# Key and query projections as seven half-size products, and another schedule for the modulation columns, in an encoder layer on one core

## The chip, the cores and the metric

The kernel runs on one core of a Trainium2 chip. The metric is the device time of one execution in microseconds (us). A profiled execution comes with it: a trace of every instruction, and a page that sums it up. Engines: PE multiplies matrices (PEld loads its stationary operand), DVE is the vector engine, ACT the scalar engine, POOL is GpSimd, SP issues loads.

## The reference, cut to what matters

One layer on 512 tokens of width 1024: a SwiGLU block (FFN1), a mixer, a second SwiGLU block (FFN2). Each begins with an RMS norm whose output is scaled and shifted by vectors made from `c`.

```python
mod = c_act @ w_mod[l] + b_mod[l]
(sh1, sc1, g1, sh2, sc2, g2, sh3, sc3, g3) = jnp.split(mod, N_MOD, axis=-1)
...
h = modulate(rmsnorm(x, norm_mix[l]), sh2, sc2)
qa, ka, va, qb, kb, vb, ga, gb = jnp.split(h @ w_in[l], SPLIT_POINTS, axis=-1)
...                                     # attention A: windowed, on qa, ka, va
qb = apply_rope(rmsnorm(qb.reshape(B, S, B_HEADS, 2, HEAD_DIM), qn_b[l]), cos, sin)
kb = apply_rope(rmsnorm(kb.reshape(B, S, B_HEADS, 2, HEAD_DIM), kn_b[l]), cos, sin)
ob = diff_attention(qb, kb, vb, lam)    # attention B: dense, difference of two softmaxes
...
merged = jax.nn.sigmoid(ga) * ya + jax.nn.sigmoid(gb) * yb
x = x + g2[:, None, :] * (merged @ w_out[l])
```

## The kernel before

All products are done in three passes: each float32 operand is split into a high and a low part (`split_from`, line 190: a cast on ACT and a subtraction on DVE), and high x high, high x low and low x high are added up in PSUM. A weight tile is 128 x 1024 (512 KB); it comes into one of five `raw` buffers, and its parts go to one of five slots of two large tiles, `high` and `low` (`high_low`). For some weights the low part is made otherwise: ACT writes minus the high part, and a load from POOL's queue adds the weight to it (`load_main`).

**FFN1 and FFN2** use Winograd's form of Strassen's scheme, in class `Unit`: a product of 2 x 2 blocks with seven products of half size in place of eight. Four differences of h blocks (`h_sum`: `n1`, `n2`, `t3`, `t4`) and three sums of weight blocks are needed; the latter are made by accumulating loads on POOL's queue. Each product (`a11`, `a12`, `s1`, `s2`, `s3`, `s4`, `a22`) is 4 chunks x 2 halves x 3 matmuls of 256 columns (`two`, lines 458 to 460). `Unit.after` copies and adds the products to the four result blocks `c11`, `c12`, `c22`, `c21` and hands each to `post`. `run_items` runs a list of such products, and asks for and splits their weights some products ahead (`ASK`, `MAKE`).

**The modulation vectors** are made in columns of 128 values: a 512 KB load of `w_mod`, and one multiply-and-reduce on DVE (`mod_col`, line 283). `column` loads one and computes the one loaded two or so calls before. 24 columns (`rest`) run beside FFN1, a column whenever `SIDE` = 0.27 an item has added up to 1; 24 (`later`) beside the mixer's projections, one in four steps; 8 (`latest`) beside the last product of the mixer.

**The mixer** begins with `boundary`: the end of FFN1, the norm in two halves (`hidden`, lines 354 to 363) and three gates' products with their matmuls. Then `main()` yields PE's steps one by one: the projections of B's values, keys and queries (`project`, lines 1202 to 1204: 8 chunks x 4 blocks of 128 tokens x 3 matmuls of 512 columns each), two gates, A's keys, values and queries (`project_pairs`), the other gates (`gates`) until attention B is done, then A's start, the remaining gates and the branches. Beside these steps an object `line` runs the attention's pieces when their estimated time is due (`line.at`, `line.helped`): norm and rotation of the heads (`head_stats`, `rope`), their turning on PE (`turn_heads`, four transposes), scores (`diff_scores`), softmax differences, outputs. The first scores of B wait for the second turned block of queries. The engines' order in the mixer is chosen by the scheduler of the programming layer, by program order and an estimate of what is ready; in other stages the order of some engines is as written (`manual_schedule`).

Of the kernel before, what the change touches and what calls it, by code (L numbers as in the profile page):

```python
# [11 lines left out]
F32 = mybir.dt.float32  # L12
# [100 lines left out]
EARLY, NEXT, SIDE, LATER = 3, 3, 0.27, 4  # L113
# [21 lines left out]
def layer(ctx: ExitStack, tc: tile.TileContext, a: dict):  # L135
# [212 lines left out]
    def hidden(rb, c, sc, sh, hi, lo, r=FULL[0], value=None):  # L348
# [3 lines left out]
        if value is not None:  # L352
            rb = rb[:, r]
# [3 lines left out]
        if value is not None:  # L357
            if r.stop - r.start == T:
                t3 = t.rearrange("p (t q) -> p t q", t=2)
            else:  # L360
                t3 = t.unsqueeze(1)
            S.activation(value, t3, AF.Identity, bias=s)
# [9 lines left out]
    def boundary(parts, g, norm, sc, sh, hh, hl, into, ahead, at):  # L372
# [16 lines left out]
        def h_steps(rs, r):  # L389

            before = None
# [69 lines left out]

    class Unit:
# [15 lines left out]
        in_order, by_columns, asides = (), (), {}  # L478
# [17 lines left out]
        def prepare(self, q):  # L496
# [8 lines left out]
            else:  # L505
                hi, lo = high_low(n, self.asides.get(q, ASIDE), (self, q))
# [9 lines left out]
        def multiply(self, q, ks=None):  # L516
# [6 lines left out]
            for js in ((0,), (1,)) if q in self.by_columns else (range(2),):  # L523
                for k in ks:
                    x = self.operand(OPERAND[q], k)
                    two(po, self.ready[q], k, x, new and k == 0, k == self.depth - 1, js)
# [22 lines left out]
    def run_items(items):  # L549

# [21 lines left out]
        for n, (u, q, ks, also) in enumerate(items):  # L572
# [3 lines left out]
            u.multiply(q, ks)  # L576
# [25 lines left out]
    def h_sum(t):  # L602
# [4 lines left out]
        h_op[t] = [u4() for _ in range(2)] if t == "n1" else b8()  # L607
# [3 lines left out]
        for i in range(2):  # L611
            v = hq[t][:, i * T : (i + 1) * T].rearrange("p (k q) -> p k q", k=2)
            o = h_op[t][i] if t == "n1" else h_op[t][:, 2 * i : 2 * i + 2, :]
# [223 lines left out]
    rest, later, latest = rest[: EARLY * NC], rest[EARLY * NC : (EARLY + NEXT) * NC], rest[(EARLY + NEXT) * NC :]  # L837
# [117 lines left out]
    def item1(u, q, ks=None):  # L955
        items1.append((u, q, ks, side1))

    credit, asked = [0.0], []
# [13 lines left out]
    def side1(n=SIDE):  # L972

        while small_loads and len(rest) < 20:
# [150 lines left out]
    def load_main(src, aside=0):  # L1125

        raw = sbuf("raw", [P, 1024], F32, RAW)
        nc.sync.dma_start(raw, src)
# [41 lines left out]

    vb_w = boundary(
# [19 lines left out]
    def project(srcs, n, then):  # L1191
# [3 lines left out]
        for u in range(NC // per):  # L1195
            wh, wl = srcs.pop(0) if isinstance(srcs, list) else load_halves(srcs[u])
# [54 lines left out]
    def head_stats(raw, nh, rs, scale8):  # L1251

        sq = f2()
        n = nh * HD
        S.activation(sq[:, 0:n], raw, AF.Square)
        V.tensor_reduce(rs, sq[:, 0:n].rearrange("p (h d) -> p h d", d=HD), axis=AX.X, op=ALU.add)
        if scale8:
            V.tensor_scalar(rs, rs, HD * EPS, None, ALU.add)
        else:
            V.tensor_scalar(rs, rs, 1.0 / HD, EPS, ALU.mult, ALU.add)  # L1260
        G.tensor_tensor(rs, rs, half[:, 0:nh], ALU.pow)
        return sq

    def rope(raw, nh, tabs, t, z):
        C, R = tabs
        n = nh * HD
        y = f2()
        r3 = raw.rearrange("p (h d) -> p h d", d=HD)
        y3 = y[:, 0:n].rearrange("p (h d) -> p h d", d=HD)
        z3 = z[:, 0:n].rearrange("p (h d) -> p h d", d=HD)  # L1270
        V.tensor_tensor(y3, r3, C[:, t, :].unsqueeze(1).broadcast_to([P, nh, HD]), ALU.mult)
        for o, i in ((slice(0, NF), slice(NF, HD)), (slice(NF, HD), slice(0, NF))):
            V.tensor_tensor(z3[:, :, o], r3[:, :, i], R[:, t, o].unsqueeze(1).broadcast_to([P, nh, NF]), ALU.mult)
# [845 lines left out]
```

## Time and profile before

| | |
|---|---|
| median of 3 runs | 1034.36 us (1034.01 to 1039.83) |
| profiled execution | 1034.51 us, its span 1032.7 us |
| PE busy | 1027.6 us, 7346 matmuls |
| DVE busy | 787.4 us |
| ACT busy | 582.1 us |
| POOL busy | 161.8 us |
| moved by DMA | 220.39 MB |
| mean granted clock of PE | 0.999 |

The span goes from the first to the last instruction; the execution's time holds some 2 us around it. FFN1 lies at 0 to 340 us, the boundary to 373.6, values, keys and queries to 439.9, attention B from 466 to 563, attention A from 570 to 641, FFN2 from 709 on.

### The profile page before, as it was taken

The numbers are of one execution on the slowest core, as the hardware profiler recorded it, in microseconds if no ns is written. First come the engines' busy times: TensorE is split into PE (matmuls) and PEld (weight loads), VectorE is DVE, ScalarE is ACT, GpSimd is POOL, SyncE is SP. The second block draws the span as 40 slices with busy tenths as digits, with TensorE's granted clock in tenths as the row PEclk, the third lists the DMA queues.
The fourth block names the chain that finished last, engine by engine and source line by source line (L and its number), as shares of the span: only waits on it lengthen the run. The fifth ranks groups of instructions, "written<-read, shape, count | busy, mean of one in ns | idle before, by whom it ended". The sixth has DMA issues, their size and how long they took to land.

```text
span 1032.7 us, 18848 instructions
## 1 busy us (share of the span) xinstructions
PE 1027.6 (100%) x7346; PEld 949.0 (92%) x7346; DVE 787.4 (76%) x1457; ACT 582.1 (56%) x1013; POOL 161.8 (16%) x189
## 2 busy tenths in 40 slices
PE   9999999999999999999999999999999999999998
PEld 7889899899998998899888888989999999999998
DVE  7886667567787679859772588976898777877877
ACT  6755335244454443668785856525877556655553
POOL 1101110110100100543323101001112112212210
PEclk9999999999999999999999999999999999999999
DMA  9977887967875459796737944974498998989974
GB/s 363 371 207 202 239 241 219 251 153 243 218 188 158 144 213 410 237 281 135 181 79 185 259 136 151 367 250 103 93 239 195 238 236 209 222 228 215 207 158 113
DMA packets 70233, 220.39 MB, mean 213 GB/s; under 512 B 8448, under 2 KB 13184, under 8 KB 70144
## 3 DMA queue, kind: packets, MB, share of 16 engines
q1 hardware_dynamic: 47808, 146.52, 39.2%
q0 software_dynamic: 19200, 68.17, 35.9%
q10 hardware_dynamic: 3136, 4.51, 1.2%
q8 instruction: 57, 0.93, 0.4%
q14 instruction: 32, 0.26, 0.1%
HBM read 208.94 MB, written 10.23 MB: 212 GB/s over the span
## 4 chain that ended last, share of the span: by engine, by line
PE 96%; DVE 2%; ACT 2%; issue 0%; POOL 0%; DVEq 0%; ACTq 0%
PE acc L460 7%; PE acc L459 7%; PE acc L458 7%; PE sc L460 6%; PE sc L458 6%; PE sc L459 6%; PE sc L174 5%; PE sc L176 5%; PE sc L175 5%; PE acc L174 5%; PE acc L176 5%; PE acc L175 5%; PE tp L1281 2%; PE acc L709 2%; PE acc L1203 2%; PE acc L1202 2%
## 5 line engine op out<-in xcount | busy, mean ns | idle before, releaser
L190 ACT CAST high<-raw 128x1024 fp32r<-128x1024 f32 (+2 forms) x176 | 158.4, 914 | 149.4 <-PE sc L175 40.8
L190 DVE TENSOR_TENSOR low<-raw,high 128x1024 fp32r<-128x1024 f32 (+2 forms) x176 | 183.5, 1052 | 40.4 <-ACT high L190 38.8
L459 PE MATMUL acc<-b,high 128*128 128x256 f32 x508 | 140.5, 277 | 0.1
L458 PE MATMUL acc<-b,high 128*128 128x256 f32 x508 | 140.6, 277 | 0.0
L460 PE MATMUL acc<-b,low 128*128 128x256 f32 x508 | 140.5, 277 | 0.0
L460 PE MATMUL sc<-b,low 128*128 128x256 f32 x500 | 138.0, 276 | 0.0
L458 PE MATMUL sc<-b,high 128*128 128x256 f32 x500 | 138.0, 276 | 0.0
L459 PE MATMUL sc<-b,high 128*128 128x256 f32 x500 | 138.0, 276 | 0.0
L190 ACT CAST high<-u 128x1024 fp32r<-128x1024 f32 (+1 forms) x73 | 75.4, 1034 | 52.3 <-PE sc L175 20.0
L190 DVE TENSOR_TENSOR low<-u,high 128x1024 fp32r<-128x1024 f32 (+1 forms) x73 | 87.7, 1201 | 21.5 <-ACT high L190 20.0
L174 PE MATMUL sc<-b,high 128*128 128x512 f32 (+1 forms) x272 | 97.4, 358 | 0.0
L175 PE MATMUL sc<-b,high 128*128 128x512 f32 (+1 forms) x272 | 97.0, 357 | 0.0
L176 PE MATMUL sc<-b,low 128*128 128x512 f32 (+1 forms) x272 | 97.0, 357 | 0.0
L459 PEld LDWEIGHTS acc<-b,high 128*128 128x128 f32 x508 | 95.4, 188 | 0.5 <-DVE b L1903 0.3
L458 PEld LDWEIGHTS acc<-b,high 128*128 128x128 f32 x508 | 95.4, 188 | 0.2
L460 PEld LDWEIGHTS acc<-b,low 128*128 128x128 f32 x508 | 95.4, 188 | 0.1
L460 PEld LDWEIGHTS sc<-b,low 128*128 128x128 f32 x500 | 93.9, 188 | 0.0
L458 PEld LDWEIGHTS sc<-b,high 128*128 128x128 f32 x500 | 93.9, 188 | 0.0
L459 PEld LDWEIGHTS sc<-b,high 128*128 128x128 f32 x500 | 93.9, 188 | 0.0
L174 PE MATMUL acc<-b,high 128*128 128x512 f32 (+1 forms) x240 | 89.2, 372 | 0.0
L176 PE MATMUL acc<-b,low 128*128 128x512 f32 (+1 forms) x240 | 86.6, 361 | 0.0
L175 PE MATMUL acc<-b,high 128*128 128x512 f32 (+1 forms) x240 | 86.5, 360 | 0.0
(400 smaller groups left out, 2717.9 us busy)
## 6 DMA issues: line engine op xcount, KB each, us to landing
u<-w_mod SPq DMA_DIRECT2D x38, 512.0 KB, 8.0
b<-w_mod SPq DMA_DIRECT2D x32, 512.0 KB, 5.5
raw<-w2i SPq DMA_DIRECT2D x31, 512.0 KB, 5.6
u<-w2i POOLq DMA_DIRECT2D x31, 512.0 KB, 6.8
raw<-w1u SPq DMA_DIRECT2D x24, 512.0 KB, 6.5
u<-w1u POOLq DMA_DIRECT2D x24, 512.0 KB, 7.1
raw<-w1o SPq DMA_DIRECT2D x24, 384.0 KB, 4.8
raw<-w_gate SPq DMA_DIRECT2D x16, 512.0 KB, 5.4
```

The source lines that it names most:

```text
L174: PE.matmul(out, wh, xh, start=first, stop=False)
L175: PE.matmul(out, wh, xl, start=False, stop=False)
L176: PE.matmul(out, wl, xh, start=False, stop=last)
L190: last = S.copy(hi, src), V.tensor_tensor(lo, src, f(hi), ALU.subtract)
L458: PE.matmul(out, wh[:, s], xh, start=first and j == 0, stop=False, skip_group_check=True)
L459: PE.matmul(out, wh[:, s], xl, start=False, stop=False, skip_group_check=True)
L460: PE.matmul(out, wl[:, s], xh, start=False, stop=last and j == 1, skip_group_check=True)
L709: PE.matmul(out1[i][:, r], w[:, i * P : (i + 1) * P], h[:, r], start=first and r.start == 0, stop=last and r.stop == T, skip_group_check=True,
L1202: PE.matmul(out[t][:, 0:n], hh[k][:, ht], wh[:, o : o + n], start=k == 0, stop=False)
L1203: PE.matmul(out[t][:, 0:n], hh[k][:, ht], wl[:, o : o + n], start=False, stop=False)
L1281: PE.transpose(tp[:, j * P : (j + 1) * P], src, ident)
```

## The change

Two things are changed together.

Keys and queries of attention B become two `Unit`s (`projected`), each with seven products of half size. Here h is the stationary operand and the weight the moving one (`two_turned`). Their weights are laid out in four blocks, whose sums are made by accumulating loads; the four differences of h are made on DVE and ACT beside the values' projection, from f32 values of h that ACT now keeps in the boundary (`hidden` with `value`). The result blocks, two blocks of tokens by four heads, go through `two_blocks` (which attention A used before) in place of `head_stats` and `rope`, and are turned a quarter at a time (`turn_quarter`). The first scores wait for all four key quarters and the first query quarter; later ones for the query quarter that they read. `item_steps` is `run_items` as a generator, so that columns and attention pieces can come between its products' parts. SP's order from the values to the first two gates is as written.

The columns: 32 beside FFN1 at 0.44 an item, none beside the items of the final out products and of the last unit; 4 (`later`) beside the values (one in 8 steps) and the units (one in 14); 12 (`tail`) beside the gates from the tenth turned block of attention B on, one in four steps, into `raw` buffers, with the activated `c` loaded anew into one of these; 8 (`latest`) as before.

```diff
-EARLY, NEXT, SIDE, LATER = 3, 3, 0.27, 4
+EARLY, NEXT, SIDE, LATER = 4, 2, 0.44, (8, 14, 2)
+BESIDE_V = 4
...
             for c in range(NC):
-                h = hidden(rs, c, sc, sh, hh[c], hl[c], r)
+                value = hq[f"b{c // 4 + 1}{n}"][:, c % 4 * H : (c % 4 + 1) * H]
+                h = hidden(rs, c, sc, sh, hh[c], hl[c], r, value)
...
+    def two_turned(po, w, k, x, first, last, js=range(2)):
+
+        (wh, wl), (xh, xl) = w, x
+        s = slice(k * 2 * P, (k + 1) * 2 * P)
+        for j in js:
+            r = slice(j * P, (j + 1) * P)
+            out = po[:, j * H : (j + 1) * H]
+            PE.matmul(out, xh[:, r], wh[:, s], start=first and j == 0, stop=False, skip_group_check=True)
+            PE.matmul(out, xl[:, r], wh[:, s], start=False, stop=False, skip_group_check=True)
+            PE.matmul(out, xh[:, r], wl[:, s], start=False, stop=last and j == 1, skip_group_check=True)
...
     def item1(u, q, ks=None):
-        items1.append((u, q, ks, side1))
+        ended = u.final if isinstance(u, Out1) else u.p == NH - 1
+        items1.append((u, q, ks, lambda: side1(0.0 if ended else SIDE)))
...
-            w = room[len(columns) % len(room)] if columns is not later else None
-            asked.append((v, c, mod_load(v, c, w)))
+            w = None
+            if columns is tail:
+                w = sbuf("raw", [P, 1024], F32, RAW)
+            elif columns is not later:
+                w = room[len(columns) % len(room)]
+            with tc.issue_after(loaded[0]) if columns is tail else nullcontext():
+                asked.append((v, c, mod_load(v, c, w)))
         if asked and (len(asked) > COLUMNS[columns is rest] or not columns):
-            mod_col(*asked.pop(0), in_order=columns is not later)
+            after = summed[0] if columns is later else split[1] if columns is tail else None
+            with nullcontext() if after is None else tc.issue_after(after):
+                mod_col(*asked.pop(0), in_order=columns is rest or columns is latest)
...
+    def projected(w, post, odd):
+        u = Unit([w[i] for i in range(4)], 4, h1_operand, post, odd)
+        u.srcs = dict(zip(("a11", "a12", "a21", "a22"), u.srcs))
+        u.products, u.aside = two_turned, -ASIDE
+        u.in_order = ("s1", "s2", "s3", "s4", "a22")
+        return u
...
+    key_unit.ask("s1")
     vb_w = boundary(
...
+    def keys_b(c, v, u):
+        n, i, raw = quarter(c, v)
+        rs = small(8)
+        y = two_blocks(raw, 4, table["kb"], i, rs.rearrange("p (t h) -> p t h", t=2), False)
+        y3 = y.rearrange("p (h d) -> p h d", d=HD)
+        V.tensor_tensor(y3, y3, rs.unsqueeze(2).broadcast_to([P, 8, HD]), ALU.mult)
+
+        def turn():
+            turn_quarter(y, n, i, kb_h, kb_l)
+            keys_done.add((n, i))
+
+        line.at(line.helped(3.2, 4.0) + SLACK, turn, ("tp",))
...
     def main():
-        yield from beside(project(vb_w, T, values_b), LATER)
-        yield from beside(project(a["w_kb"], T, keys_b), LATER)
-        yield from beside(project(a["w_qb"], T, queries_b), LATER)
-        yield from beside(gates(lambda: gate_next[0] < EARLY_A), 1)
+        with tc.manual_schedule(engines={mybir.EngineType.SP}):
+            k, q = key_unit, query_unit
+            with tc.issue_after(split[0]), tc.issue_after(split[1]):
+                k.prepare("s1")
+            h_sum("n1", False)
+            for t in ("n2", "t3", "t4"):
+                h_sum(t, False)
+            summed.append(split[1])
+            for p in ("a11", "a12"):
+                k.ask(p)
...
+            yield from beside(project(vb_w, T, values_b, also), LATER[0])
+            items = [(k, p, None, None) for p in ("s1", "a11", "a12", "s2", "s4", "s3")]
+            items += [(q, "s1", None, None), (k, "a22", None, None)]
+            items += [(q, p, None, None) for p in ("a11", "a12", "s2", "s4", "s3", "a22")]
+            yield from beside(item_steps(items, MM3), LATER[1])
+            yield from beside(gates(lambda: gate_next[0] < EARLY_A), LATER[2])
...
-        yield from gates(lambda: done["b"] < NT)
+        yield from gates(lambda: turns["b"] < 10)
+        cact[0] = sbuf("raw", [P, 1024], F32, RAW)
+        with tc.issue_after(loaded[0]):
+            nc.sync.dma_start(cact[0], c_scr.partition_broadcast(P))
+        yield from beside(gates(lambda: done["b"] < NT), 4, tail)
+        while tail or asked:
+            column(tail)
         line.drain(lambda: done["b"] == NT)
         start_a()
```

More of the change, by code (lines that the diff above doesn't have):

```diff
@@ L549, in run_items, with item_steps @@
     def run_items(items):
+        for _ in item_steps(items):
+            pass
+    def item_steps(items, cost=None):
         due, at, now = [], [], 0.0
@@ L1249, in gates @@
             gate_end(j, out)
[L1251 to L1273, printed above, removed]
-        V.tensor_tensor(y[:, 0:n], y[:, 0:n], z[:, 0:n], ALU.add)
-        return y
     def turned(srcs, tag="tp"):
@@ L1287, in cut @@
         return [src[:, j * P : (j + 1) * P] for j in range(n)]
-    def turn_heads(y, nt, t, hi, lo, then=None):
-        ht = slice(t * P, (t + 1) * P)
-        v = turned(cut(y, nt)).rearrange("p (j q) -> p j q", j=nt)
-        with tc.high_priority():
-            split_from(hi[:, 0:nt, ht], lo[:, 0:nt, ht], v)
-        turns["t"] = t + 1
-        if then is not None:
-            line.at(line.free["tp"] + SLACK, then, SCORES)
     def raws(ps, n=T):
```

119 lines of the change are left out of this document (72 added, 47 removed).

## The prediction

> **What bounds the kernel now.** I read the page first: the busy shares and the chain that ended last. Then the waits of the tensor engine (PE), which tell whether a busy PE is also an unhindered one.
>
> ```profile
> span 1032.7 us, 18848 instructions
> PE 1027.6 (100%) x7346; PEld 949.0 (92%) x7346; DVE 787.4 (76%) x1457; ACT 582.1 (56%) x1013; POOL 161.8 (16%) x189
> ...
> PE 96%; DVE 2%; ACT 2%; issue 0%; POOL 0%; DVEq 0%; ACTq 0%
> ```
> ```profile
> PE acc L634 <- DVE sm L640: 0.9, 1, 0.9
> PE acc L187 <- DVE u L190: 0.2, 1, 0.2
> ```
>
> Look at two things: the chain lies on PE for 96% of the span, and the whole list of PE's waits adds up to 1.1 us (one at the start, one near 601 us in the window attention). Busy time alone would not prove that PE streams at its peak, because matmuls overlap. So I take the spacing of their starts, first of the three projections with 512 columns (values, keys, queries in a row), then of matmuls with 256 columns.
>
> ```profile
> 373.61 0.40 PE L1202 MATMUL sc<-high,b 128*128 128x512 f32 x1
> ...
> 439.90 0.39 PE L174 MATMUL acc<-b,high 128*128 128x512 f32 x1
> ```
> ```profile
> 451.63 0.28 PE L1222 MATMUL acc<-high,b 128*128 128x256 f32 x1
> ...
> 453.84 0.28 PE L1223 MATMUL acc<-low,b 128*128 128x256 f32 x1
> ```
> ```profile
> 820.00:880.00 60.00, 60.00 (x531) 60.00 (x531) 46.21 (x68) 33.96 (x49) 11.28 (x13) 1.00 0.93 225
> ```
>
> The code issues 8 chunks x 4 blocks x 3 = 96 matmuls for each projection, so 288 start between 373.61 and 439.90, with two groups of four transposes among them (0.44 us and a little each): (66.29 - 1.1) / 288 = 0.2264 us each. In the last row, of a stretch of FFN2 (columns: PE, PEld, DVE, ACT, POOL, clock, DMA share, GB/s), 531 matmuls of 256 columns touch 60 us, some two of them overhanging: 60 / 529 = 0.1134 us. That is half of 0.2264, with the granted clock at 1.00. Between lie the `L1222` group's rows: from 451.63 to 453.84 are 19 starts, 0.1163 us each. So the kernel is bound by the number of columns that PE streams, and the stage of this change stands in an unbroken stream.
>
> **The change part by part.**
>
> *Seven products for eight.* Removed: keys and queries, 192 matmuls x 0.2264 = 43.5 us. Added: two units of 7 products x 4 chunks x 2 halves x 3 = 168 matmuls of 256 columns, 336 in all. In them h is stationary and the weights move, as in `L1222`, but with the banks and operand tiles of the FFN units. Bounds: 336 x 0.1134 = 38.1 and 336 x 0.1163 = 39.1 us. I take 0.115, between the two, since the trace has both: 38.6 us. That is -4.9 us (bounds -5.4 and -4.4). The transposes stay 32 in number, in eight groups of four.
>
> The Trainium skill ("TensorE: Matmul & The Clock Gate", "Back-to-back issue gap") speaks against this: it gives a sustained spacing of about 81 ns at 128 columns and 131 ns at 512, so short matmuls would pay more for each column. An estimate by that page, 98 ns at 256 columns on the line between, makes 336 x 0.098 = 32.9 us against 192 x 0.131 = 25.2: 7.8 us slower. By that rule, the trace does not agree: 0.1134 is half of 0.2264.
>
> *What DVE and ACT get for it.* The units need four sums of h (two subtractions and two splits on DVE each), 14 weight splits for 8, and 6 additions of the quarters.
>
> ```profile
> 368.47 4.63 DVE L190 TENSOR_TENSOR low<-raw,high 128x1024 fp32r<-128x1024 f32 x4 [0.45 <-ACT high L190]
> ...
> 407.21 1.29 DVE L190 TENSOR_TENSOR low<-raw,high 128x512 fp32r<-128x512 f32 x2
> 408.42 1.28 DVE L283 CUSTOM_DVE_ANT_0 u<-u,ka,par 128x1024 f32<-128x1024 f32 x1
> ```
> ```profile
> 374.00:396.00 22.00, 22.00 (x99) 18.20 (x98) 16.75 (x29) 4.97 (x10) 0.00 (x0) 1.00 1.01 389
> 396.00:418.00 22.00, 22.00 (x99) 18.23 (x98) 19.33 (x38) 7.93 (x16) 0.00 (x0) 1.00 1.03 409
> 418.00:440.00 22.00, 22.00 (x102) 18.18 (x102) 20.45 (x42) 15.55 (x30) 13.19 (x8) 1.00 0.65 199
> 440.00:466.00 26.00, 26.00 (x181) 24.02 (x180) 14.49 (x36) 17.18 (x33) 10.78 (x8) 1.00 1.05 281
> ```
>
> Two 512-wide operations take 1.21 us from start to start (407.21 to 408.42), a full weight split 1.16 (4.63 / 4). Added: 16 x 0.605 = 9.7 for the sums, 14 x 1.16 - 8 x 1.21 = 6.6 for the splits, 6 x 0.605 = 3.6: 19.9 us. Removed from this stretch: 20 of the 24 modulation columns at 1.28, 25.6 us. DVE falls from 71.0 us (the four rows) to about 65, while PE's 92 us fall to 87. So on average DVE has room. Within the units it is tighter; one tile's norm and rotation stand in a row here, an operation of each kind:
>
> ```profile
> 427.23 0.68 DVE L1274 TENSOR_TENSOR f<-f,f 128x512 f32<-128x512 f32 x1
> ...
> 430.36 0.69 DVE L190 TENSOR_TENSOR low<-raw,high 128x512 fp32r<-128x512 f32 x1
> ```
>
> That is 430.36 - 427.23 = 3.1 us, and 0.6 for the split of the turned tile (queries have one multiplication less): 3.7 a key quarter, 3.1 a query quarter. Beside the 38.6 us of products come 11 weight splits (three are made during the values), 12.8; additions, 3.6; the values' own four splits, 2.4; two columns, 2.6; four key and two query quarters, 14.8 + 6.2: 42.4 us. What lags is the rotation, which nothing needs before the first scores. Forecast cost 0.3 us; bounds 0 and 3.8 (all of the overhang shown as PE waits). Queued behind a late split on DVE would be the next split, and behind that PE's next product; behind a late POOL accumulation, the one that turns one weight sum into the next.
>
> ```profile
> u<-w1u POOLq DMA_DIRECT2D x24, 512.0 KB, 7.1
> ```
> ```profile
> 420.38 3.72 POOL L1261 TENSOR_TENSOR sm<-sm,half 128x8 f32<-128x8 f32 x2 [60.33 <-DVE sm L1260]
> ```
>
> Eight accumulating loads join POOL's queue, each 7.1 us to landing by the row of FFN1, among the eight powers of the norms, 1.9 us each (3.72 / 2). The products that read them come at least three products (8 us) after the split that releases them, the spacing at which FFN1 and FFN2 run without a PE wait. Nothing more for them, inside the same bounds. SP's order in this stretch is now the program's, past the loads of the removed columns: at 389 to 409 GB/s they filled the DMA engines, and without 10 MB of them the eight accumulations have room.
>
> *Boundary.* Before the mixer, ACT keeps an f32 value of h too: 16 more activations of 256 columns.
>
> ```profile
> 366.20 0.51 ACT L355 ACTIVATE b<-f,mod 128x256 fp32r<-128x256 f32 x1 [0.28 <-DVE f L354]
> 366.99 0.51 ACT L355 ACTIVATE b<-f,mod 128x256 fp32r<-128x256 f32 x1 [0.28 <-DVE f L354]
> ```
>
> A step takes 0.79 us, ACT is idle for 0.28; a second activation of at most 0.51 makes it at most 1.02, 0.23 x 8 = 1.8 us later at the end of a half. The second half's work goes under the gates' matmuls, and the first weight split of the values ends at 368.47 + 1.16 = 369.6, with 4.0 us to the start of their matmuls at 373.61. The chain through the norm of the second half is shorter of slack. I take 0.3 us, bounds 0 and 1.8.
>
> *Columns.* FFN1 takes 32 for 24, at 0.44 an item for 0.27, and none beside its last out products and its last unit.
>
> ```profile
> 80.00:160.00 80.00, 80.00 (x560) 74.27 (x559) 55.85 (x74) 33.85 (x44) 9.66 (x11) 1.00 0.88 233
> 160.00:240.00 80.00, 80.00 (x563) 74.37 (x562) 54.24 (x70) 33.59 (x43) 7.92 (x9) 1.00 0.71 188
> 240.00:317.00 77.00, 77.00 (x585) 73.22 (x584) 59.82 (x92) 37.79 (x52) 8.48 (x10) 1.00 0.80 227
> ...
> 744.00:798.00 54.00, 54.00 (x479) 54.00 (x478) 50.22 (x82) 38.70 (x67) 11.30 (x13) 1.00 0.95 220
> ```
>
> DVE: 169.9 us of 237, plus 8 x 1.28 = 10.2: 76%. FFN2 has DVE at 50.22 / 54 = 93% and PE unbroken, so this costs nothing; without that cover, 10.2 us is what could show. The loads bring 8 x 0.5 MB, 10 us at 409 GB/s, into a stage whose DMA share is 0.80 on average. Taking columns from FFN1's end gains nothing: no PE wait stands there.
>
> Twelve columns go beside the end of the differential attention: 15.4 us of DVE, and 6.3 MB, 15.4 us at 409 GB/s.
>
> ```profile
> 500.00:535.00 35.00, 34.94 (x215) 28.17 (x215) 27.52 (x73) 30.08 (x78) 12.28 (x18) 1.00 0.47 114
> 535.00:570.00 35.00, 35.00 (x196) 29.50 (x193) 12.47 (x33) 22.13 (x55) 8.85 (x14) 1.00 0.72 174
> ```
>
> DVE has 30 us free in these 70, the DMA engines 28 (0.53 x 35 + 0.28 x 35). They fit; cost 0, and the far end is in the rivals.
>
> *Earlier attention.* The first scores stand at
>
> ```profile
> 466.43 0.74 PE L187 MATMUL sc<-b,b 64*128 64x512 f32 x3
> ```
>
> and need now one query quarter and all keys, ready ten products after the values' end (373.6 + 21.7 + 27.6 = 422.9) plus about 8 us of norm and rotation: near 432. That gives no time by itself (PE had work anyway); it leaves more gate matmuls as cover for the window attention, worth the 0.2 us wait at 601.
>
> **Sum**, against the profiled execution's own 1034.51 us (span 1032.7): 1034.5 - 4.9 + 0.3 + 0.3 - 0.2 = 1030.0 us. The median shown is 1034.36, 0.15 less, so 1029.8.
>
> **The rivals.**
>
> *Gate weights starve (slower).* The tail's columns load into the five buffers that gate weights pass through; the activation vector holds one of them, and up to three columns are in flight, so one or two are left.
>
> ```profile
> raw<-w_gate SPq DMA_DIRECT2D x16, 512.0 KB, 5.4
> low<-w_gate POOLq DMA_DIRECT2D x13, 512.0 KB, 7.1
> ```
> ```profile
> 427.48 1.15 ACT L1134 ACTIVATE low<-raw 128x512 fp32r<-128x512 f32 x2
> 428.53 1.13 ACT L1132 CAST high<-raw 128x512 fp32r<-128x512 f32 x2
> ```
>
> A gate's weights hold a buffer for 5.4 us and ACT's four half-casts after it (two from 427.48 to 428.53, so 2.1 us): 7.5 us. A gate is 24 x 0.2264 = 5.4 us of PE, some 7 with the attention's pieces. With one buffer, and loads that wait for each other, that is up to 7.5 + 7.1 - 7 = 7.6 us late for a gate when also the accumulation isn't hidden, and the tail spans about six. It decides once the two or three gates loaded ahead are used up; three late ones by half of this are 11 us: 1041. Against it: attention and its end come some 30 us earlier, so fewer than six gates may run beside columns. Chance 0.08.
>
> *DVE becomes the bound in the units.* 42.4 against 38.6, all shown in place of the 0.3: 1029.8 + 3.5 = 1033.3. For it: DVE at 93% (20.45 of 22) where queries are projected already. Against: nothing needs the lagging part soon. Chance 0.14.
>
> *Half-size matmuls bound by weight loads.* Twice as many loads for each column: if each took its own time,
>
> ```profile
> L459 PEld LDWEIGHTS acc<-b,high 128*128 128x128 f32 x508 | 95.4, 188 | 0.5 <-DVE b L1903 0.3
> ```
>
> 188 ns, 336 would take 63.2 us, 19.7 more than now: 1054. The FFN2 row (531 in 60 us) says that loads overlap. The rule quoted above is of this kind. Chance 0.02.
>
> *The saving does not arrive* (waits of other kinds around the units take it back): 1034.4. Chance 0.06.
>
> **How the numbers follow.** Forecast 1029.8, chance 0.70; its own range 1027.8 (all bounds at their good ends: 1034.4 - 5.4 - 0.2 = 1028.8, and 1 us for the spread between runs) to 1032.5. The whole range goes to the DVE rival, the lost saving and the lesser part of the starving gates: 1027.8 to 1036.5. One per cent, about 10.3 us, is what a measurement of this kernel tells from no change. Faster by over 1% would take more than twice the saving of the products: 0.02. Slower by over 1% (above 1044.7): the weight-load rival and the worst of the starving gates, 0.05. The rest, 0.93, within 1%.
>
> **What would show it.** The two units should take 38 to 39 us from the first to the last of their 336 matmuls, spaced at 0.113 to 0.117 us; PE's waits should still be a list of 1 to 3 us; the first scores should stand near 432 us, the twelve columns between 490 and 570. A wrong forecast would show as PE waits on DVE splits or accumulating loads in the units, on gate weights before the window attention, or as a spacing of 0.12 us or more.

## The result, and the profile after

The changed kernel takes 1085.5 us (median of 4 runs, 1081.6 to 1087.7) where the kernel before, run beside it, takes 1034.8: a ratio of 1.048, 95% interval 1.044 to 1.052. The forecast was 1029.8, its range 1027.8 to 1036.5. It was wrong in sign and by 56 us.

First the page of the changed kernel: span, busy shares, two rows of its forty slices (busy tenths of PE, and the clock granted to it), and the chain that ended last.

```profile
span 1083.5 us, 19194 instructions
...
PE 1040.6 (96%) x7490; PEld 961.1 (89%) x7490; DVE 804.7 (74%) x1477; ACT 597.1 (55%) x1035; POOL 168.6 (16%) x197
...
PE   9999999999999999999966799999999999999998
...
PEclk9999999999999999999986899999999999999999
...
PE 74%; DMA 8%; DVE 8%; ACT 5%; issue 3%; POOL 1%; SPq 0%; DVEq 0%; ACTq 0%; POOLq 0%
```

PE's share of the chain fell from 96% to 74%; DMA, DVE and ACT now stand in it. The hole is in slices 21 to 23 (27.1 us each), 542 to 623 us: the end of attention B and the start of A. There the clock drops as well. PE's waits, a list of 1.1 us before, begin like this:

```profile
PE acc L177 <- DMA low<-w_gate: 13.5, 4, 4.8
PE tp L1302 <- DVE b L191: 7.0, 1, 7.0
```

Four gates waited for their weights, 13.5 us in total. The same stretches as before (columns: PE, PEld, DVE, ACT, POOL, clock, DMA share, GB/s):

```profile
500.00:535.00 35.00, 32.87 (x234) 28.63 (x233) 26.21 (x66) 21.55 (x52) 10.26 (x11) 0.95 0.27 76
535.00:570.00 35.00, 25.25 (x117) 20.26 (x115) 13.16 (x30) 10.04 (x31) 7.80 (x10) 0.90 0.64 179
570.00:600.00 30.00, 20.45 (x75) 15.48 (x76) 6.70 (x14) 17.25 (x33) 10.09 (x12) 0.72 1.00 279
```

Before, PE was busy for 69.94 of the 70 us from 500 to 570; now for 58.1, and no other engine is busier over these 70 us than before. No engine is overloaded there: they wait for each other. PE also runs below its full clock, most of all from 570 to 600 (0.72).

Where the time came in, read from the first and last matmuls of each stage (us from the span's start):

| | before | after | later by |
|---|---|---|---|
| last half-size product of FFN1 | 321.2 | 325.3 | 4.1 |
| values begin | 373.6 | 379.3 | 5.7 |
| keys and queries end | 439.7 | 447.7 | 8.0 |
| first scores of B | 466.4 | 442.8 | -23.6 |
| last scores of B | 535.1 | 522.3 | -12.8 |
| first scores of A | 570.2 | 602.9 | 32.7 |
| FFN2 begins | 709.4 | 758.0 | 48.6 |
| FFN2 ends | 1028.8 | 1078.9 | 50.1 |

Attention B came earlier, as forecast. Its last scores stood 12.8 us ahead; 80.6 us later, where before it took 35.1, came A's first.

### The profile page after: what moved, and what is told of

It is laid out like the page before. It is cut to its first block, busy times and chain, and to the rows that moved or that the text cites. A ratio compares the mean times of both kernels' runs of the same rounds, so it can differ in the third digit from the quotient of the medians.

```text
span 1083.5 us, 19194 instructions
## 1 busy us (share of the span) xinstructions
PE 1040.6 (96%) x7490; PEld 961.1 (89%) x7490; DVE 804.7 (74%) x1477; ACT 597.1 (55%) x1035; POOL 168.6 (16%) x197
## 4 chain that ended last, share of the span: by engine, by line
PE 74%; DMA 8%; DVE 8%; ACT 5%; issue 3%; POOL 1%; SPq 0%; DVEq 0%; ACTq 0%; POOLq 0%
PE acc L458 6%; PE acc L457 6%; PE acc L459 6%; PE sc L457 6%; PE sc L459 6%; PE sc L458 6%; PE sc L176 4%; PE sc L175 4%; PE sc L177 4%; PE acc L177 3%; PE acc L175 3%; PE acc L176 3%; DMA raw<-w_gate 2%; DMA low<-w_gate 2%; PE acc L730 2%
## 5 line engine op out<-in xcount | busy, mean ns | idle before, releaser
L191 DVE TENSOR_TENSOR low<-u,high 128x1024 fp32r<-128x1024 f32 (+1 forms) x76 | 91.2, 1201 | 23.5 <-ACT high L191 22.1
L191 ACT CAST high<-u 128x1024 fp32r<-128x1024 f32 (+1 forms) x76 | 78.6, 1034 | 53.8 <-PE sc L176 13.9
L177 PE MATMUL acc<-b,low 128*128 128x512 f32 (+1 forms) x240 | 90.1, 376 | 13.5 <-DMA low<-w_gate 13.5
L175 PE MATMUL acc<-b,high 128*128 128x512 f32 (+1 forms) x240 | 92.2, 384 | 3.8 <-ACT high L1167 3.8
L176 PE MATMUL acc<-b,high 128*128 128x512 f32 (+1 forms) x240 | 89.9, 375 | 0.0
```

The source lines that it names most:

```text
L175: PE.matmul(out, wh, xh, start=first, stop=False)
L176: PE.matmul(out, wh, xl, start=False, stop=False)
L177: PE.matmul(out, wl, xh, start=False, stop=last)
L191: last = S.copy(hi, src), V.tensor_tensor(lo, src, f(hi), ALU.subtract)
```

## The experiments

Eighteen kernels were run: first the parts apart, then what is behind each part. "Before" was 1034.6 to 1035.3 us beside them. The diffs show the lines that matter; to leave columns out or move them, the kernels also change the loops that ask for them.

### The parts apart

**Units with the old columns** (24 beside FFN1, 24 beside the projections, none at the attention's end).

```diff
-EARLY, NEXT, SIDE, LATER = 4, 2, 0.44, (8, 14, 2)
-BESIDE_V = 4
+EARLY, NEXT, SIDE, LATER = 3, 3, 0.27, (4, 4, 1)
+BESIDE_V = 24
```

> The change's projections with the columns of before (24 beside FFN1 at 0.27 an item, 24 beside the mixer's start, one in four steps, none in raw buffers). Theory (the twelve tail columns hold the raw buffers, gate weights come late, and everything behind ACT's wait with them): no loss in the tail; the saving of the products, 4.9 us, less up to 4 us where DVE is now fuller in the units: 1030 to 1034 us. Rival (the units bring the attention forward into A's norms and so overload DVE and ACT): the loss stays, over 1060 us.

1070.6 us, ratio 1.036 (1.033 to 1.038): the rival. The units stretch ends at 470.1 in place of 439.7.

**The new columns with the old projections.** Only the lists of columns, `item1` and `column` are the new ones.

```diff
-EARLY, NEXT, SIDE, LATER = 3, 3, 0.27, 4
+EARLY, NEXT, SIDE, LATER = 4, 2, 0.44, 8
+BESIDE_V = 4
```

> The projections of before, the columns as changed: 32 beside FFN1 at 0.44, 4 beside the values, 12 in raw buffers beside the end of attention B. Theory (raw buffers): FFN1 loses about 4 us and the tail some tens: 1060 to 1085 us. Rival (the units' earlier attention): little beside FFN1's 4 us: about 1039 us.

1072.8 us, 1.039 (1.036 to 1.042), as the theory had it. So each half of the change costs over 35 us by itself, and the halves were taken apart further.

**Units without any column beside the mixer.**

```diff
-(EARLY * NC, EARLY * NC + BESIDE_V), (EARLY * NC + BESIDE_V, (EARLY + NEXT) * NC),
+(0, 0), (0, 0),
```

> The change's projections, FFN1 with its 24 columns as before; the 24 columns of the mixer (gate 2, scale 3, shift 3) are left out, their bias stands for them, so nothing of them loads or runs. Theory (the units themselves cost what was worked out, and it is the column loads that come in their way on SP's written order): the saving arrives, 1029 to 1031 us. Rival (the units are late by their own accumulating loads, PSUM copies and DVE's share, whatever the columns do): 1040 us or more.

1041.6 us, 1.007 (1.006 to 1.008): the rival. The seven products lose time even alone.

**FFN1's columns alone** (32 at 0.44, none at its end; 16 beside the old projections), from the kernel before:

```diff
-EARLY, NEXT, SIDE, LATER = 3, 3, 0.27, 4
+EARLY, NEXT, SIDE, LATER = 4, 2, 0.44, 5
+BESIDE_V = 16
...
+        ended = u.final if isinstance(u, Out1) else u.p == NH - 1
+        items1.append((u, q, ks, lambda: side1(0.0 if ended else SIDE)))
```

> The kernel of before, and of the change only this: 32 columns beside FFN1 at 0.44 an item, none at its end, 16 beside the projections, no tail. Theory (a reduction at the head of DVE's queue waits for its load, and the weight splits behind it with it): FFN1 4 to 5 us later, the rest as before: 1038 to 1041 us. Rival (such waits are hidden by weights made ahead): 1034 to 1035 us.

1041.1 us, 1.006 (1.005 to 1.008), the theory's upper end.

**The tail's columns alone** (12 beside the end of attention B, 12 beside the old projections), from the kernel before:

```diff
-EARLY, NEXT, SIDE, LATER = 3, 3, 0.27, 4
+EARLY, NEXT, SIDE, LATER = 3, 3, 0.27, 7
+BESIDE_V = 12
...
+        yield from beside(gates(lambda: done["b"] < NT), 4, tail)
```

> The kernel of before, and of the change only this: twelve of the mixer's 24 columns go to the end of attention B through the raw buffers (the other twelve beside the projections, one in seven steps); FFN1 as before. Theory (raw buffers held by columns make gate weights late): 30 us or so of the 38 that the changed columns cost by themselves: 1060 to 1070 us. Rival (in columns_alone it was FFN1's columns that put the attention off its times): under 1045 us.

1061.0 us, 1.026 (1.024 to 1.027), as the theory had it. The three parts alone, +7 and +6.5 and +26.4 us, make 40 of the 50.7. Of the other 11, some 5 show without any units: FFN1's columns and the tail cost 38.2 together, and 32.9 one by one. The rest shows only when columns and units stand side by side.

### The tail

SP's and DVE's rows in order of time, in the changed kernel, show how it comes about:

```profile
456.78 0.50 SPq L246 DMA_DIRECT2D raw<-w_mod  x1
...
467.08 0.33 SPq L246 DMA_DIRECT2D raw<-w_mod  x1
475.53 0.33 SPq L1163 DMA_DIRECT2D raw<-w_gate  x1
493.06 9.13 SPq L246 DMA_DIRECT2D raw<-w_mod  x2
529.18 0.33 SPq L1163 DMA_DIRECT2D raw<-w_gate  x1
```
```profile
527.93 1.22 DVE L284 CUSTOM_DVE_ANT_0 raw<-raw,raw 128x1024 f32<-128x1024 f32 x1
```

Column loads were issued at 456.8, 467.1, 493.1 and 501.9, and the first reduction ran at 527.9, in DVE's order right behind a split of the attention. The fifth buffer had held the activated vector since 454.0. So from 501.9 to 527.9 all five `raw` buffers were taken and none was left for a gate. Columns are reduced in the order of their loads, so the first one kept its buffer for 71 us. The next gate's load waited in SP's queue (488 to 560 us):

```profile
SPq L1163 <- DVE mod L295: 27.2, 1, 27.2
```

What follows is a ring. The rows below, of one stretch of all engines, show its second half:

```profile
558.12 0.76 PE L177 MATMUL acc<-b,low 128*128 128x512 f32 x1 [4.81 <-DMA low<-w_gate]
...
559.96 0.84 PE L1302 MATMUL tp<-ident,x 128*128 128x128 f32 x3
...
562.07 1.27 DVE L284 CUSTOM_DVE_ANT_0 raw<-raw,raw,par 128x1024 f32<-128x1024 f32 x1
...
563.38 0.33 SPq L1163 DMA_DIRECT2D raw<-w_gate  x1
```

A gate's load, issued at 538.8 when a column had been reduced, landed at 545.7; ACT's casts followed until 549.6, and the accumulating load for its low part landed at 558.0. PE stood 4.8 us before that gate, with a turn of the attention behind it in its order. The turn released ACT's cast (at 560.8), the cast DVE's split (at 561.5), and the next reduction was tied behind this split. Only then did a buffer come free for another gate's load, at 563.4. That is 24.6 us for one turn of the ring, and a gate is 5.4 us of PE.

Attention A starts late for a second reason. The first load of its queries (`qa_scr`) was issued at 581.8, behind five gates' loads, and landed 14.5 us later; before, it was issued at 540.1 and landed after 2.6 us. The turn that waited 7.0 us (until 611.8) stood behind a split whose cast on ACT came after 8.1 us of waiting for a branch's weights.

**No tail** (its 12 columns beside the values and units instead).

```diff
-EARLY, NEXT, SIDE, LATER = 4, 2, 0.44, (8, 14, 2)
-BESIDE_V = 4
+EARLY, NEXT, SIDE, LATER = 4, 2, 0.44, (4, 5, 2)
+BESIDE_V = 16
...
-        yield from beside(gates(lambda: done["b"] < NT), 4, tail)
+        yield from gates(lambda: done["b"] < NT)
```

> The changed kernel with the twelve tail columns moved beside the values and units (16 there), so none goes through raw buffers; FFN1 as changed. Theory (raw buffers): the 40 us of the mixer's second half are gone, FFN1's loss of 4 to 5 us stays: 1033 to 1038 us. Rival (the units' earlier attention): over 1070 us.

1063.3 us, 1.028 (1.027 to 1.030): neither. From the last scores of B to the first of A it is 42 us again in place of 80.6, but the units with 16 columns now end at 470.9.

**The tail's reductions untied.**

```diff
-after = summed[0] if columns is later else split[1] if columns is tail else None
+after = summed[0] if columns is later else None
```

> The changed kernel; the tail's reductions on DVE are no longer tied to the last split written. Theory in a narrower form (a buffer is held long because the reduction waits behind a split of the attention): the holding falls from 26 us to some 5, most of the tail's 40 us goes: 1045 to 1055 us. Theory in its plain form (three of five buffers are too many, whenever they come free): over 1070 us.

1073.4 us, 1.036 (1.031 to 1.041), with runs from 1064.2 to 1076.6: 12.1 us came back, less than the narrower theory's 30 to 40. By the number it is the plain form (over 1070), but the trace gives another reason. The holding did fall: a column is reduced 3.5 to 13.8 us after its load's issue. But the first reduction, no longer tied, now stood in DVE's order before a load that had not landed, with the softmax of B behind it and PE behind that:

```profile
473.42 1.22 DVE L284 CUSTOM_DVE_ANT_0 raw<-raw,raw 128x1024 f32<-128x1024 f32 x1 [8.46 <-DMA raw<-w_mod]
```
```profile
PE acc L188 <- ACT x L1404: 7.6, 1, 7.6
```

From 460 to 500 us PE was busy for 28.7 of 40 us here, and for 39.9 in the changed kernel. So the edit gave back some 23 us in the tail (an estimate: 12.1 + 11.2) and lost 11 in front of it.

**The kernel before with the tail, one load in flight, untied.**

```diff
-if asked and (len(asked) > COLUMNS[columns is rest] or not columns):
+if asked and (len(asked) > (0 if columns is tail else COLUMNS[columns is rest]) or not columns):
```

> The kernel before with the twelve tail columns, but one load in flight in place of three, and a reduction no longer tied behind the attention's last split. Theory: the 26 us of the tail come from the buffers that waiting columns take from the gate weights: with one column in flight and released at once, 1036 to 1046 us. Rival: the reductions themselves, or the load of the activated vector into a buffer, delay the attention's end: it stays above 1052 us.

1044.7 us, 1.008 (1.006 to 1.011), against 1061.0: 16.3 of the 26.4 us, as the theory had it. No gate waits for weights any more:

```profile
PE tp L1295 <- DVE u L191: 4.2, 5, 1.2
PE tp L1295 <- DVE ka L191: 2.6, 1, 2.6
```

The same twelve columns, reductions and reloaded vector remain, but a column is now reduced 3.5 to 12.1 us after its load's issue, where the first took 76 us with the tail alone. So most of the tail's price is how long a column keeps its buffer. Of the 10 us that are left, 6.8 show as these small waits for splits.

**The changed kernel with this edit.**

> The changed kernel with one tail column in flight in place of three, its reduction not tied behind the attention's last split. In the kernel before with the tail alone the same edit gave back 16 us. Theory: the tail costs the changed kernel through the same buffers, so the same comes back: 1064 to 1072 us. Rival: in the changed kernel attention stands some 25 us earlier, and the gates' weights are late for other reasons: above 1078 us.

1071.1 us, 1.038 (1.033 to 1.042), with runs from 1069.2 to 1080.1: 14.4 us back, as the theory had it by the number. Untying alone gave 12.1 of these, so no effect of the count in flight shows beyond the spread; in the kernel before, the two edits weren't run apart. The new wait of DVE and PE before 475 us is here too (PE busy for 29.2 of the 40 us from 460 to 500), so the tail itself costs the changed kernel more than the 14.4 us.

### FFN1

DVE's waits from 80 to 330 us hold, in the changed kernel:

```profile
DVE b L284 <- DMA b<-w_mod: 9.6, 5, 2.7
```
```profile
PE sc L459 <- DVE low L191: 1.1, 2, 0.6
```

DVE's reductions stand in program order, and five times one stood there, its load not landed, with splits behind it. PE, which waited for nothing in this stretch before, now stands before such splits (second view, the same stretch; 2.8 us of waits in all), and FFN1 ends 4.1 us later. DVE's average of 76% says nothing of that. With these columns alone, 5.0 us are lost by the end of FFN1 in the profiled execution and some 2.4 in FFN2; the latter wasn't traced to a cause.

**The same 32 columns, evenly to FFN1's end.**

```diff
-EARLY, NEXT, SIDE, LATER = 4, 2, 0.44, 5
+EARLY, NEXT, SIDE, LATER = 4, 2, 0.37, 5
```

> The kernel before with 32 columns beside FFN1 (16 beside the projections), spread evenly to FFN1's end at 0.37 an item, in place of 0.44 with none at the end. Theory: a column asked for every 6.2 us finds its load not landed and holds DVE up; at one in 7.4 us the loads land in time: 1034 to 1036.5 us. Rival: what costs is the number of columns (DVE work and 4 MB of loads more), not their rate: 1039 to 1042 us.

1042.4 us, 1.006 (1.004 to 1.008): the rival by the time, but the trace shows two causes. DVE's waits on these loads halved (5.3 us, 4 times; with the columns at 0.44 alone, 10.3), and up to 310 us PE lost 1.7 us in place of 4.9. The loss moved to the end, where columns now stood beside the loads of the weights for FFN1's last out products (`w1o`), here in SP's order:

```profile
PE sc L175 <- ACT high L191: 3.8, 1, 3.8
```
```profile
313.72 0.33 SPq L246 DMA_DIRECT2D b<-w_mod  x1
314.14 1.33 SPq L921 DMA_DIRECT2D raw<-w1o  x3
```

Before, these loads stood in SP's queue from 301.1 on with no column between. So by the trace the rate sets the first loss and the loads at the end the second; neither spread of the eight columns was free.

### Columns beside the units

With the old columns beside the units, PE's and (365 to 470 us) SP's greatest waits are these, with two rows of SP in order of time:

```profile
PE acc L177 <- ACT f L1520: 9.0, 1, 9.0
```
```profile
SPq L246 <- DVE mod L284: 55.1, 16, 9.7
```
```profile
399.87 11.67 SPq L246 DMA_DIRECT2D u<-w_mod  x3
415.75 0.33 SPq L502 DMA_DIRECT2D raw<-w_qb  x1
```

SP spends half of the stretch in front of column loads whose buffers wait for reductions; a unit's weight (`L502`) stands behind them. Also, these columns' reductions stay tied behind the last difference of h: the first one runs at 387.8, in the kernel before at 377.0. No run changed that.

**The loads placed by the scheduler in this stretch.**

```diff
-        with tc.manual_schedule(engines={mybir.EngineType.SP}):
+        with nullcontext():
```

> The units with 24 columns beside them as in units_old_columns (1070.6 us), but SP's order in this stretch is chosen by the scheduler, not as written. Theory (unit weights wait behind column loads, which wait for a buffer until a reduction has run): 1035 to 1050 us. Rival (DVE or POOL is full, the order of the loads doesn't matter): 1065 us or more.

1064.1 us, 1.028 (1.027 to 1.030): 6.5 us of 36, so the written order is the lesser part.

**One column load in flight in place of two**, in the written order again.

```diff
-if asked and (len(asked) > COLUMNS[columns is rest] or not columns):
+if asked and (len(asked) > (0 if columns is later else COLUMNS[columns is rest]) or not columns):
```

> Units with the columns of the kernel before beside them (24 of them), but one column load in flight in place of two. Theory: the 29 us that these columns cost beside the units, on top of the 7 of the units, come from buffers that columns hold while the units' weights need them: with one fewer held, 1050 to 1062 us. Rival: they come from the written order of the loads, where a unit's weight stands behind columns: no better than 1066 us.

1063.3 us, 1.026 (1.024 to 1.028): 7.3 us, between the theories. If the two add up, which no run tested, held buffers and order carry some 7 each; what carries the other 15 wasn't separated.

### The units by themselves

Why does even the kernel without columns lose 7 us? Distances from each matmul's start to the next one's, added up by the kind of the first, from the values to FFN2, before and in the units without columns:

| | before | units, no columns |
|---|---|---|
| keys and queries | 43.8 | 41.5 |
| transposes | 22.5 | 26.1 |
| scores | 22.2 | 23.7 |
| gates and branches, 512 columns | 129.4 | 131.0 |
| A's projections | 34.6 | 35.7 |
| all else | 83.4 | 83.8 |
| sum | 335.8 | 341.8 |

The products save 2.3, and what stands among and behind them loses 8.3.

**The first scores of B held back** until A's keys and values are projected.

```diff
-SCORES + (lambda: len(keys_done) == 4,)
+SCORES + (lambda: len(keys_done) == 4 and held,)
...
         yield from project_pairs([a["w_kva"][u] for u in range(2)], keys_a, True)
+        held.append(1)
```

> Keys and queries as seven products, FFN1 as before, the mixer's 24 columns left out (the bias stands for them), and the first scores of attention B held back until A's keys and values are projected, about where the kernel before has them. Theory: the units are nearly sound by themselves, and the 7 us that they cost come from turns and scores of attention B between the products of the second unit, where each waits for DVE or ACT: with those moved back, 1031 to 1035 us. Rival: the units and what they need from DVE and ACT cost this wherever attention stands: 1039 to 1043 us.

1044.7 us, 1.009 (1.006 to 1.011): the rival, and 1.7 us above its range. From 372 to 470 us the turns' waits were small and stayed so (1.1 us with and without the edit), which speaks against the theory; one for a gate came:

```profile
PE acc L177 <- DMA low<-w_gate: 6.0, 1, 6.0
```

**The same with the loads placed by the scheduler**, and **the units without columns with the loads placed by it** (the edit shown above):

> As the run with the scores held back (units, FFN1 as before, the mixer's 24 columns left out), but the loads of the stretch are placed by the scheduler in place of the written order. With the scores held back, the turns' waits had gone, and one wait of 6.0 us for a gate's weights stood in their place. Theory: that wait comes from the written order, which puts the gates' loads behind all those of the units; without it the units show their saving: 1030 to 1036 us. Rival: it comes from ACT and POOL, which handle the gate's weights behind the units' pieces in their order: 1040 to 1045 us, the wait for the gate's weights still there.

> Units, FFN1 as before, the mixer's 24 columns left out, scores of attention B not held back, and the loads of the stretch placed by the scheduler. Theory: the 7 us of the units come from turns and scores that wait for DVE and ACT between the products, so the loads' order changes nothing: 1039 to 1043 us. Rival: the loads' order costs most of it: 1030 to 1036 us.

1044.1 us, 1.009 (1.007 to 1.010), the 5.9 us wait still there; and 1044.4 us, 1.009 (1.007 to 1.010). So the loads' order isn't it. POOL's rows in order of time, of the kernel before and then of the one with the scores held back, show where that gate's weights are late:

```profile
428.94 0.95 POOL L1135 DMA_DIRECT2D low<-w_gate  x1 [2.02 <-ACT low L1134]
```
```profile
431.06 1.74 POOL L1526 TENSOR_TENSOR rqb<-rqb,half 128x8 f32<-128x8 f32 x1 [5.33 <-DVE rqb L1523]
432.75 1.81 POOL L1169 DMA_DIRECT2D low<-w_gate  x2
```

Before, the first gate's accumulating load is issued at 428.9 and lands at 437.4; PE comes to it after 439.7. With the units it is issued at 432.8, behind a norm's power that waited 5.3 us for DVE, and behind ACT's casts, which end there too; it lands at 442.6. PE stands before it from 436.3. PE arrives 3.4 us sooner, and the weights come 5.2 us later. It arrives sooner also because PE's order, which the scheduler chose, has this gate's first matmuls (the third of them waited until 442.63) in front of the last product of the units:

```profile
443.65 0.41 PE L468 MATMUL acc<-high,b 128*128 128x256 f32 x1
```

The 24 matmuls of that product run from 443.65 on. The last weight split in front of them ended at 434.1, and the addition `L548`, for which this product waits in the run with subtractions below, ended at 436.9; so they could probably have filled the wait. No run changed PE's order of gates and products, so this rival stands.

**The first two gates' low parts by subtraction** in place of that load.

```diff
-wh, wl = load_main(a["w_gate"][j])
+wh, wl = load_halves(a["w_gate"][j]) if j < EARLY_A else load_main(a["w_gate"][j])
```

> As the run with the scores held back (units, FFN1 as before, the mixer's 24 columns left out), but the low parts of the first two gates' weights are made by subtractions on DVE in place of ACT's second cast and an accumulating load. Theory: the 6 us wait for the first gate's weights is the chain that follows the release of a slot by a unit's product (ACT's casts from 426.8 to 432.8 us, then 9.8 us to the load's landing at 442.6); a subtraction of 1.2 us in place of the load takes the wait away: 1035 to 1040 us. Rival: DVE's and ACT's own order makes those parts as late as the load did: 1042 us or more.

1042.7 us, 1.007 (1.005 to 1.009): the rival. That wait went, and these came, among others:

```profile
PE tp L1301 <- DVE b L191: 1.9, 1, 1.9
PE acc L468 <- DVE f L548: 1.4, 1, 1.4
```

**The rotation of B's keys and queries left out** (of its three steps, the first multiplication stays), without columns and with early scores.

```diff
+        if not rotate:
+            return y
         for o, q in ((slice(0, NF), slice(NF, HD)), (slice(NF, HD), slice(0, NF))):
```

> Units, FFN1 as before, the mixer's 24 columns left out (the bias stands for them), and for B's keys and queries the two multiplications by the sine table and the addition of the rotation left out as well: 11.0 us less on DVE between 400 and 450 us (16 x 0.416 + 7 x 0.683 us in the trace of the units without columns), where DVE is busy for 19.9 of the 20 us from 410 to 430. Theory: DVE is the bound in the units; what waits there (turns, splits, the next gate's weights) comes in time, and the time falls to 1030 to 1036 us. Rival: slots, ACT and the turns' own chain set the waits: 1039 us or more.

The stretch from 410 to 430 with the rotation and, below, without it:

```profile
410.00:430.00 20.00, 19.71 (x168) 19.37 (x167) 19.89 (x35) 12.48 (x20) 7.64 (x5) 1.00 0.47 106
```
```profile
410.00:430.00 20.00, 17.88 (x140) 17.51 (x139) 15.50 (x23) 10.85 (x17) 7.62 (x5) 0.91 0.47 106
```

1048.4 us, 1.012 (1.010 to 1.014): slower, though DVE had room now (the work left out adds up to 11.4 us by the numbers of the expectation, not 11.0). The turn at 424.2 had waited 2.1 us for a split, and the clock was halved from there for 3.41 us. Why it is slower wasn't separated; that the amount of DVE's work alone is the bound is refuted.

**The turns 8 us later in PE's order.**

```diff
-line.at(line.helped(3.2, 4.0) + SLACK, turn, ("tp",))
+line.at(line.helped(3.2, 4.0) + 8.0 + SLACK, turn, ("tp",))
```

> As the run with the scores held back and the first two gates' low parts from subtractions (units, FFN1 as before, the mixer's 24 columns left out), but each turn of a key or query quarter stands 8 us later in PE's order. In that run PE stood 2.0 us at 433.9 and 2.0 us at 447.4 before a turn, 1.5 us at 440.8 before a product, and 1.4 us went to a halved clock behind. Theory: PE works in its order, and a turn placed before its tile is ready stops the products behind it; placed later, these waits go: 1034 to 1039 us. Rival: the late thing behind it (a product's weights or its result bank) shows then: 1041 us or more.

1042.9 us, 1.008 (1.006 to 1.009): the rival. Next late were A's first weights:

```profile
PE acc L1269 <- DMA low<-w_kva: 3.8, 1, 3.8
```

They landed at 445.5, 2 us sooner than before (447.5), but PE wanted them at 441.4 instead of 451.3, since its order now has A's first projections in front of most of the gates' matmuls. None of these six edits gave time back against the 1041.6 us; most moved the wait. Shown is that in PE's order something that isn't ready stands behind the units each time. Whether PE's own order, ACT's, POOL's or the five slots set that is open.

## Why the prediction was wrong, point by point

*The products*, -4.9: the right direction. In the changed kernel the first and the last of the 336 are

```profile
401.09 0.28 PE L468 MATMUL sc<-high,b 128*128 128x256 f32 x1
...
447.65 0.28 PE L470 MATMUL acc<-low,b 128*128 128x256 f32 x1
```

with a median spacing of 0.117 us, just above the upper bound (0.1163). Counted from each start to the next, waits included, they take 42.8 us (41.5 without columns), where 38.6 was forecast and 43.8 stood before. The rule quoted with this term from the Trainium skill ("TensorE: Matmul & The Clock Gate", "Back-to-back issue gap") would have made them 7.8 us slower; the trace doesn't agree, also at twice the count of short matmuls: 0.117 is little more than half of 0.2264.

*DVE in the units*, +0.3, bounds 0 to 3.8: the term failed. It compared sums of busy time (42.4 against 38.6) and said that nothing needs the lagging part soon. PE works in its order, and turns, gates and A's projections stand right behind. The term named DVE alone; the waits found go through DVE, ACT, POOL and PE's own order, at +7 for -4.9, so 12 us off. Which of these sets the 7 us stays open. *The saving does not arrive* named this outcome at 1034.4 and was 7 short.

*Boundary*, +0.3: without the new FFN1 it took 52.9 us for 52.4, within its bounds. *Earlier attention*, -0.2: the first scores came at 436.7 without columns, forecast near 432, and gave no time.

*FFN1's columns*, 0 "costs nothing": measured +6.5 alone, 5.0 of it by the end of FFN1. FFN2's 93% on DVE was the wrong comparison: there DVE's work is at hand, here it waits in order for a load.

*The tail*, 0 because DVE and the DMA engines had room: the step that failed most, +26.4 alone. Room on engines was not what the columns use up. The rival *Gate weights starve* had the buffers, the gates and the right place, and priced three late gates at 11 us, with a chance of 0.08. It counted on up to three columns in flight and one or two buffers left; four columns were loaded before the first was reduced, and none was left. Left out were PE's order, in which the attention's turns stand behind a late gate, the reduction tied behind a split, which closes the ring, and the clock.

*The clock* was no term at all. In the changed kernel it was halved from 529.1, 556.4, 570.1 and 607.6 on, for 3.41, 6.83, 17.07 and 10.24 us. Against full speed the matmuls in these took some 9 us more: at most a fifth of the whole loss, as some of it may lie in front of waits that would have come anyway.

## What to carry to other kernels

Before work is moved into an idle engine's time, ask what it holds while it waits: a column that costs 1.2 us of DVE kept a buffer for up to 71 us, and the buffer was the bottleneck. A saving on the bounding engine counts only if what stands next in its order is ready sooner: look up when each next operand lands, in time, not in busy shares. In an in-order queue a wait costs what stands behind it; follow one late item through every queue until it comes back to the first.

## What the runs showed of the hardware

The granted clock is halved for 3.41 us or multiples of it (3.41, 6.83, 10.24 and 17.07 us above), and a wait of 1.9 us can be enough. In the run with the gates' low parts by subtraction (PE in order of time):

```profile
449.70 0.66 PE L1301 MATMUL tp<-ident,f 128*128 128x128 f32 x4 [1.87 <-DVE b L191]
...
450.82 0.63 PE L175 MATMUL acc<-b,high 128*128 128x512 f32 x1
```

After this wait and four transposes, such matmuls take 0.63 us where they take 0.39 from 454.0 on, and start 0.43 apart for 0.23, from 450.4 for 3.41 us; that cost 1.4 us more. What tells most cases apart is how busy PE was in the 3.41 us just before. In the changed kernel:

```profile
525.71:529.12 3.41, 1.86 (x12) 1.20 (x11) 3.21 (x11) 3.41 (x10) 0.00 (x0) 1.00 0.00 0
542.77:546.18 3.41, 1.54 (x7) 1.31 (x8) 0.00 (x0) 0.51 (x1) 0.00 (x0) 1.00 0.72 275
```

The clock was halved behind the first row (PE busy for 1.86 us), not behind the second (1.54 us); behind 0.30, 1.32 and 0.56 us, before the other three halvings, it was. Cut into such stretches, the traces of all twenty kernels have no halving of a full clock behind more than 1.9 us of busy PE, and none left out behind less than 1.5; in between both occur. The Trainium skill ("TensorE: Matmul & The Clock Gate", "Why this matters for your kernels") advises against idle gaps of over some 3 us. By these traces, shorter ones can halve the clock when they fall into one such stretch.
